# Group 0's first norm in pairs of feature tiles, with later mix loads and another home for the first projection weights

## The chip, the cores and the metric

The kernel runs on one core of one Trainium2 chip. The metric is the device time of one launch in microseconds (us); lower is better. Only one execution is profiled; the other runs give a time alone.

## The reference, cut to what matters

One layer of a streaming encoder is computed for 1024 prompt frames and 32 frames of a running stream, model width 1024. In short:

```
h   = x * (1 + sc1) + sh1                       # adaLN, sc/sh/g from the conditioning vector
... = split(h @ w_in)                           # q,k,v and gates of three head groups
mix = concat([mlstm, fox, gmlp]) @ w_o          # 4 + 8 + 4 heads of 64
x   = layer_norm(ALPHA * x + (1 + g1) * mix, ln1_g, ln1_b)
h   = x * (1 + sc2) + sh2
y   = (silu(h @ w_gate) * (h @ w_up)) @ w_down
x   = layer_norm(ALPHA * x + (1 + g2) * y, ln2_g, ln2_b)
```

All matrices are float32. The kernel works with features on the 128 partitions and frames along the free axis, so a vector of 1024 features is 8 feature tiles. It also returns keys, values, gates and states.

## The kernel before, in words

**Split products.** A float32 product is made of three matmuls (`gemm`, L111): each operand is kept as a rounded high half and a low half (hi, lo), and hi*hi, hi*lo and lo*hi are added up in PSUM. `weights` (L92) loads 512 KB of weights into one of three `raw` buffers, casts the high half on ScalarE (L104) and subtracts for the low half on VectorE (L105); the halves `whi` and `wlo` go into rings of three buffers each in the common pool `wp`, or into a pool that the caller names.

**Groups.** The frames are two groups: group 0 is frames 0 to 511, group 1 is frames 512 to 1055, the 32 stream frames last. Each group is cut into two column ranges (`MM`); for group 0 they are 0 to 255 and 256 to 511, called the first and the second range below.

**Order of the work.** After the start come the projections and the mixing heads of group 0, in an order written out by hand (`ORDER`, L42). Its last entries are the projection of attention head 7 for group 0 (`q7`, `head_unit`, L396), chunk 2 of the mLSTM, the attention of head 7 (`f7`), chunk 3 of the mLSTM (`m3`) and a gMLP unit (`G3`). `head_unit` ends with four evacuations of its bank (L408 to L413) and stores of the queries and keys to DRAM (L418, L419). Then `run` emits, from L1462:

1. `wo_mix(0, ...)` for six of the eight tiles of the concatenated mix: load a tile from DRAM (SyncE queue, L1006), cast its high half on ScalarE (L1007), subtract for its low half on VectorE (L1008). The order of tiles is `KORDER[0]` = 2, 3, 4, 6, 7, 5, 0, 1; tiles 0 and 1 hold the mLSTM's heads and come last.
2. Three projections of heads 2 to 4 for group 1 (`fm_unit`, L235, with `evac_qk`, L362).
3. `wo_mix` for the last two tiles.
4. The output projection of group 0, first range, eight output tiles m in order (`wo_range`, L1045). Weights of m = 0, 1, 2 go into a pool of their own, `pw`, which takes space that the mixing heads had; those of 3 to 7 into the common ring. Residual tiles come from DRAM in pairs (`wo_res`, L1018).
5. The second range in the order 0, 5, 6, 7, 3, 4, 1, 2, with five weights kept and those of 3 and 4 made anew, woven with the norm of the first range (`ln1`, L1083).
6. The norm of the second range, three projections of heads 5 to 7 for group 1, and then the feed-forward of group 0 (`up`, L1130), woven with the attention of group 1 (`mixers`, L1330).

**The norm.** `sublayer_end` (L1065) adds gate times projection to the residual tile z (L1074) and keeps a sum and a sum of squares; the mean of feature tile 0, found by a matmul with a constant (`ln_pivot`, L928), is taken off every tile as a pivot. `ln_stats` (L972) makes a factor r and an offset e per frame. `ln1` then does, for each feature tile k: z*r (L1091) and +e (L1092) on VectorE, an affine step on ScalarE into a buffer `tmp` (ring of four) (L1095), a cast into `hh` on ScalarE (L1099), a subtraction into `hl` on VectorE (L1100). `hh` and `hl` (`tm_ah` and `tm_al` in the profile) are what `up` multiplies. The buffer `sil`, in a ring of two, is what `up` uses for its silu (L1145).

**What orders an engine's queue.** Each engine runs its instructions in one order, fixed when the program is built: the builder simulates a timeline (L1681) and takes, by the order of the code and by priority (attention and mLSTM of group 0 have a raised one, L1451), what the simulation has ready. `tc.issue_after(x)` keeps what is written inside it behind instruction x on x's engine.

Of the kernel before, what the change touches and what calls it, by code (L numbers as in the profile page):

```python
# [7 lines left out]
F32 = mybir.dt.float32  # L8
F32R = mybir.dt.float32r
AF = mybir.ActivationFunctionType  # L10
ALU = mybir.AluOpType
# [4 lines left out]
P = 128  # L16
D = 1024
KT = 8
# [8 lines left out]
MM = (((0, 256), (256, 512)), ((0, 272), (272, 544)))  # L27
# [27 lines left out]
def weave(*parts):  # L55

    parts = list(parts)
    while parts:
        for p in list(parts):
            if next(p, parts) is parts:  # L60
                parts.remove(p)


def f(ap):
    return ap.bitcast(F32)


class Kernel:
# [17 lines left out]
        return self.lastload  # L86

    def store(self, out, in_, eng=None):
        (eng or self.nc.sync).dma_start(out, in_)


    def weights(self, src, nk, ncol, eng=None, pool=None):  # L92
# [303 lines left out]
    def head_unit(self, h):  # L396

        nc = self.nc
        w = self.weights(self.d["w_in_f"][2 + h], KT, P)
        self.phase = "head"  # L400
        k1, k2, qp, q2, v = self.heads[h] = self.head_tiles(h, 512, 512)
        self.decay(q2[64:68], h, slice(2, 6), (0, 4))
        self.decay(k2[64:68], h, slice(0, 4), (0, 4))
        self.load(f(v), self.dv[:, :4, h * P:(h + 1) * P])
        ps = self.t(self.pg, [P, 512], F32, "g")
        self.gemm(ps, w, slice(0, P), *self.h1parts(0, 512))
        lo, hi = slice(0, 64), slice(64, 128)
        nc.scalar.activation(qp[lo], ps[lo], AF.Copy, scale=0.125)  # L408
        nc.vector.scalar_tensor_tensor(qp[hi], ps[lo], 0.125, f(qp[lo]), ALU.mult, ALU.subtract)
        nc.scalar.copy(k1[hi], ps[hi])  # L410
        nc.vector.tensor_tensor(k2[lo], ps[hi], f(k1[hi]), ALU.subtract)
        nc.scalar.copy(k1[lo], ps[hi])
        nc.scalar.activation(q2[lo], ps[lo], AF.Copy, scale=0.125)  # L413
        for o in (0, 256):
            kr = self.t(self.sm, [P, 272], F32, "qkr", 2)
            nc.scalar.copy(kr[hi, :256], ps[hi, o:o + 256])
            self.store(self.d["o_kT"][h, :, o:o + 256], kr[hi, :256])
        self.store(self.dqh[h, hi, :512], f(k1[hi]))  # L418
        self.store(self.dql[h, hi, :512], f(k2[lo]))  # L419
        if h < QD:  # L420
            evac = self.evac_qk(h)
            self.phase = "fm"
            for o, n in self.ranges((1,)):
                ps = self.t(self.pg, [P, 512], F32, "g")
                self.gemm(ps[:, :n], w, slice(0, P), *self.h1parts(o, n))
                evac(o, n, ps[:, :n])
# [501 lines left out]
    def ln_pivot(self, st, z, sl):  # L928
        nc = self.nc
        ps = self.t(self.pt, [P, 512], F32, "t")  # L930
        n = sl.stop - sl.start
        nc.tensor.matmul(ps[:, :n], self.ones8, z[:, 0, sl], start=True, stop=True)
        nc.scalar.copy(st["pv"][:, sl], ps[:, :n])
        nc.vector.tensor_tensor(z[:, 0, sl], z[:, 0, sl], st["pv"][:, sl], ALU.subtract)

    def ln_sum(self, st, z, m, sl):
        nc = self.nc
# [107 lines left out]
    def wo_range(self, st, a, b, order, kept, pool):  # L1045
        nc, ko = self.nc, self.KORDER[0]
        hh, hl = self.hh[0][a], self.hl[0][a]
        st["order"] = order
        for m in order:
            self.phase = "wo0"  # L1050
            if a == 0 and m % 2 == 0:
                self.wo_res(a, b, m)
            w = kept.get(m) or self.weights(self.d["w_o"][m], KT, P, None, pool if m < 3 else None)
            if a == 0 and m in (5, 7):
                with self.tc.issue_after(self.lastload.ins):
                    for k in ((0, 4), (6, 2))[m // 7]:
                        self.wo_res(*MM[0][1], k)
            kept[m] = w
            ps = self.t(self.pg, [P, 512], F32, "g")
            self.gemm(ps[:, :b - a], [w[k] for k in ko], slice(0, P), lambda i: hh[:, ko[i], :b - a],  # L1060
                      lambda i: hl[:, ko[i], :b - a])
            self.sublayer_end(0, self.z[0], m, ps, "g1", st, a, b)
            yield

    def sublayer_end(self, c, z, m, ps, gate, st, a, b):  # L1065

        sl = slice(a, b)
        pivot = st and st["pivot"]
        less = lambda: self.nc.gpsimd.tensor_tensor(z[:, m, sl], z[:, m, sl], st["pv"][:, sl], ALU.subtract)
        if pivot and m and st["sum"]:  # L1070
            less()
        g = self.modcol(gate, m)
        for x, y, i in self.parts(c, a, b):
            self.lastz = self.nc.vector.scalar_tensor_tensor(z[:, m, x:y], ps[:, x - a:y - a], g[i], z[:, m, x:y],  # L1074
                                                             ALU.mult, ALU.add)
        if pivot and m and not st["sum"]:
            less()
        if pivot and m == 0:
            self.ln_pivot(st, z, sl)
        if st and st["sum"]:  # L1080
            self.ln_sum(st, z, m, sl)

    def ln1(self, c, st, a, b):  # L1083
        self.phase = f"lna{c}"
        nc, z, hh, hl, sl = self.nc, self.z[c], self.hh[c][a], self.hl[c][a], slice(a, b)
        r, e = self.ln_stats(st, sl)
        for k in range(KT):
            yield
            self.phase = f"lna{c}"
            zk = z[:, k, sl]  # L1090
            nc.vector.tensor_tensor(zk, zk, r, ALU.mult)  # L1091
            (nc.gpsimd if c and k % 4 == 1 else nc.vector).tensor_tensor(zk, zk, e, ALU.add)  # L1092
            h = self.t(self.p2, [P, 272], F32, "tmp", 4)[:, :b - a]
            for x, y, i in self.parts(c, a, b):
                nc.scalar.activation(h[:, x - a:y - a], z[:, k, x:y], AF.Identity, bias=self.lnb[:, k, i:i + 1],  # L1095
                                     scale=self.lng[:, k, i:i + 1])
            if c:
                self.store(self.dh[:, k, sl], h)
            nc.scalar.copy(hh[:, k, :b - a], h)  # L1099
            nc.vector.tensor_tensor(hl[:, k, :b - a], h, f(hh[:, k, :b - a]), ALU.subtract)  # L1100

    def ln1_res(self, c):

        self.phase = f"lna{c}"
        for a, b in MM[c]:
            for k in range(KT):
                zk = self.z[c][:, k, a:b]
                if RESE[c] == "p":
                    self.nc.gpsimd.tensor_scalar(zk, zk, self.colp[:, 48 + k:49 + k], self.colp[:, 56 + k:57 + k],
                                                 ALU.mult, ALU.add)  # L1110
                else:
                    self.nc.scalar.activation(zk, zk, AF.Identity, bias=self.colp[:, 56 + k:57 + k],
                                              scale=self.colp[:, 48 + k:49 + k])
# [231 lines left out]
    def run(self):  # L1345
        nc, tc, d = self.nc, self.tc, self.d
# [51 lines left out]
        sl = ExitStack()  # L1398
# [61 lines left out]
        self.p2 = self.pada = self.pool("p2")  # L1460
        self.hh, self.hl, self.z = {}, {}, {}
        self.operand(0, self.ph)  # L1462
        self.wo_mix(0, self.KORDER[0][:6])
        for h in range(QD, PRE):
            self.fm_unit(w3[2 + h], self.evac_qk(h), (1,))
        self.wo_mix(0, self.KORDER[0][6:])
# [3 lines left out]
        st = self.ln_begin(nc.vector)  # L1470
        with ExitStack() as s7:
            pw = self.pool("pw", ctx=s7)
            kept = {}
            weave(self.wo_range(st, *MM[0][0], range(KT), kept, pw))
            del kept[3], kept[4]
            weave(self.wo_range(st, *MM[0][1], (0, 5, 6, 7, 3, 4, 1, 2), kept, pw), self.ln1(0, st, *MM[0][0]))
        weave(self.ln1(0, st, *MM[0][1]))
        for h in range(PRE, 8):
            self.fm_unit(w3[2 + h], self.evac_qk(h, True), (1,))
# [10 lines left out]
        last = len(GROUPS) - 1  # L1490
        for g, (j0, nj) in enumerate(GROUPS):
# [30 lines left out]
            if g == WOB - 1:  # L1522
                st = self.ln_begin(nc.gpsimd, sum=False)
# [20 lines left out]
        for g, (j0, nj) in enumerate(GROUPS):  # L1544
# [13 lines left out]
            if g < last:  # L1558
                st = self.ln_begin(nc.gpsimd, sum=False) if g == last - 1 else None
# [3 lines left out]
        n = nj * 256  # L1563
        t = self.t(self.pz, [P, 4, n], F32R, "z0", 1)
        w = self.last_weights(((t[:, 0], t[:, 1]), (t[:, 2], t[:, 3])), (2, 3))
        act2 = dict(act)
        for half, (a, b) in enumerate(LN[1][::-1]):
# [6 lines left out]
            else:  # L1574
                h, l = (self.t(pb, [P, KT * 272], F32R, f"{x}{a}", 1) for x in ("ah", "al"))
# [117 lines left out]
```

## Time and profile before

| | us |
|---|---|
| three runs | 1363.5, 1363.7, 1365.64 |
| median of the runs | 1363.7 |
| the profiled execution: its own time | 1364.8 |
| its span, first to last instruction | 1362.7 |
| TensorE (PE) busy | 1327.6 |
| VectorE (DVE) busy | 992.2 |
| ScalarE (ACT) busy | 658.5 |
| GpSimd (POOL) busy | 227.8 |

SP is SyncE, which issues most of the DMAs; "SPq" rows are its issues. A row of the timeline has the start, the duration, the engine, the line and operation, output and inputs by the program's names, how many instructions were merged into the row and, in brackets, how long the engine had been idle and what released it. "wo_" names belong to the output projection, "lna_" to its norm, "up_" to the feed-forward, "fm_" and "head_" to the projections, "fox_" to the attention.

### The profile page before, as it was taken

How to read it: one execution, taken by the hardware profiler on the slowest of the kernel's cores; microseconds unless marked ns; L12 is line 12 of the kernel's file. 1: busy time of each engine (PE TensorE's matmuls, PEld its weight loads, DVE VectorE, ACT ScalarE, POOL GpSimd, SP SyncE). 2: the span in 40 equal slices, each digit the busy share in tenths (PEclk: the TensorE clock that was granted, in tenths of full speed). 3: DMA queues.
4: the chain of work that ended last, by engine and by line, in shares of the span. 5: the costliest groups of instructions: out<-in, count | busy, mean ns of one | idle time of the engine just before them, and what ended most of it. 6: DMA issues, size and time to landing. Idle time of an engine off the chain costs nothing.

```text
span 1362.7 us, 25189 instructions
## 1 busy us (share of the span) xinstructions
PE 1327.6 (97%) x9434; PEld 1210.1 (89%) x9434; DVE 992.2 (73%) x2127; ACT 658.5 (48%) x1312; POOL 227.8 (17%) x263
## 2 busy tenths in 40 slices
PE   7999999998999899999999999999999999999996
PEld 4898988987999777888888888999999999999995
DVE  5545654678769667786776765678988988889777
ACT  3324454455436544545445354336663554545355
POOL 0202100043234200000000000373710000000341
PEclk9999999999999899999999999999999999999999
DMA  9775555546454765454344334574596758454321
GB/s 358 257 246 164 167 193 149 179 139 197 150 188 140 202 191 173 117 156 135 105 123 119 109 105 132 155 182 124 167 254 168 201 154 222 143 173 127 98 81 66
DMA packets 120377, 221.70 MB, mean 163 GB/s; under 512 B 18740, under 2 KB 64464, under 8 KB 120256
## 3 DMA queue, kind: packets, MB, share of 16 engines
q1 hardware_dynamic: 113024, 207.55, 48.7%
q0 software_dynamic: 6032, 11.94, 5.1%
q8 instruction: 74, 1.21, 0.4%
q10 hardware_dynamic: 1200, 0.62, 0.2%
q14 instruction: 47, 0.39, 0.1%
HBM read 188.13 MB, written 51.85 MB: 176 GB/s over the span
## 4 chain that ended last, share of the span: by engine, by line
PE 86%; DVE 6%; DMA 4%; ACT 2%; issue 1%; POOL 0%; SPq 0%; DVEq 0%; ACTq 0%
PE up_g L118 5%; PE up_g L119 5%; PE up_g L117 5%; PE dn_g L117 4%; PE dn_g L119 4%; PE dn_g L118 4%; PE tm_g L284 3%; PE tm_g L285 3%; PE tm_g L286 3%; PE sup_u L119 3%; PE sup_u L117 3%; PE sup_u L118 3%; PE fox_t L819 2%; PE fm_g L117 2%; PE sup_g L118 2%; PE sup_g L119 2%
## 5 line engine op out<-in xcount | busy, mean ns | idle before, releaser
L118 PE MATMUL up_g<-tm_al,up_whi 128*128 128x512 f32 (+1 forms) x384 | 141.3, 368 | 0.5 <-DVE tm_al L1100 0.5
L117 PE MATMUL up_g<-tm_ah,up_whi 128*128 128x512 f32 (+1 forms) x384 | 141.5, 370 | 0.2
L119 PE MATMUL up_g<-tm_ah,up_wlo 128*128 128x512 f32 (+1 forms) x384 | 140.6, 366 | 0.0
L1219 ACT CAST sup_whi<-sup_raw 128x1024 fp32r<-128x1024 f32 x54 | 56.0, 1048 | 90.9 <-PE dn_u L118 47.5
L117 PEld LDWEIGHTS up_g<-tm_ah,up_whi 128*128 128x128 f32 x384 | 72.8, 190 | 12.5 <-ACT tm_ah L1099 0.6
L118 PEld LDWEIGHTS up_g<-tm_al,up_whi 128*128 128x128 f32 x384 | 73.3, 191 | 11.0 <-DVE tm_al L1100 0.7
L119 PEld LDWEIGHTS up_g<-tm_ah,up_wlo 128*128 128x128 f32 x384 | 73.3, 191 | 10.7
L792 ACT ACTIVATE fox_p<-fox_s,fox_fmx 128x384 f32<-128x384 f32 (+2 forms) x96 | 55.1, 579 | 46.7 <-DVE fox_fmx L790 38.1
L104 ACT CAST up_whi<-up_raw 128x1024 fp32r<-128x1024 f32 x50 | 52.4, 1047 | 49.7 <-PE up_g L118 18.5
L1220 DVE TENSOR_TENSOR sup_wlo<-sup_raw,sup_whi 128x1024 fp32r<-128x1024 f32 x54 | 68.2, 1267 | 10.4 <-ACT sup_whi L1219 10.3
L1074 DVE SCALAR_TENSOR_TENSOR wo_z<-dn_g,start_mod,wo_z 128x512 f32<-128x512 f32 (+4 forms) x120 | 60.3, 521 | 20.1 <-PE dn_g L119 19.8
L105 DVE TENSOR_TENSOR up_wlo<-up_raw,up_whi 128x1024 fp32r<-128x1024 f32 x50 | 65.4, 1308 | 12.1 <-ACT up_whi L104 11.4
L117 PE MATMUL dn_g<-up_acth,dn_whi 128*128 128x512 f32 (+2 forms) x200 | 74.1, 371 | 0.0
L119 PE MATMUL dn_g<-up_acth,dn_wlo 128*128 128x512 f32 (+2 forms) x200 | 73.4, 367 | 0.0
L118 PE MATMUL dn_g<-up_actl,dn_whi 128*128 128x512 f32 (+2 forms) x200 | 72.9, 365 | 0.0
L824 ACT CAST fox_pth<-fox_t 128x512 fp32r<-128x512 f32 (+1 forms) x80 | 41.1, 545 | 55.9 <-PE fox_t L819 55.8
L104 ACT CAST dn_whi<-dn_raw 128x1024 fp32r<-128x1024 f32 (+1 forms) x44 | 42.7, 970 | 51.5 <-PE dn_u L118 11.2
L787 DVE TENSOR_REDUCE fox_fmx<-fox_s 128x1 f32<-128x384 f32 (+2 forms) x96 | 52.6, 552 | 13.5 <-PE fox_s L784 12.3
L825 DVE TENSOR_TENSOR fox_ptl<-fox_t,fox_pth 128x512 fp32r<-128x512 f32 (+1 forms) x80 | 49.4, 631 | 15.7 <-ACT fox_pth L824 15.5
L105 DVE TENSOR_TENSOR dn_wlo<-dn_raw,dn_whi 128x1024 fp32r<-128x1024 f32 (+1 forms) x44 | 49.5, 1126 | 12.6 <-ACT dn_whi L104 11.8
L284 PE MATMUL tm_g<-tm_whi,start_h1h 128*128 128x256 f32 (+1 forms) x192 | 55.9, 291 | 1.8 <-DVE tm_traw L355 1.7
L285 PE MATMUL tm_g<-tm_wlo,start_h1h 128*128 128x256 f32 (+1 forms) x192 | 56.1, 292 | 0.0
(663 smaller groups left out, 4788.9 us busy)
## 6 DMA issues: line engine op xcount, KB each, us to landing
up_raw<-w_gu SPq DMA_DIRECT2D x50, 512.0 KB
dn_raw<-w_dn SPq DMA_DIRECT2D x28, 512.0 KB
ada_late<-w_ada SPq DMA_DIRECT2D x24, 512.0 KB
sup_raw<-w_gu SPq DMA_DIRECT2D x20, 512.0 KB
start_dp<-w_gu SPq DMA_DIRECT2D x19, 512.0 KB
start_dp<-w_gu POOLq DMA_DIRECT2D x19, 512.0 KB, 8.0
wo_raw<-w_o SPq DMA_DIRECT2D x18, 512.0 KB
sup_raw<-start_dp SPq DMA_DIRECT2D x18, 512.0 KB
```

Source lines behind the costliest of these rows:

```text
L104: nc.scalar.copy(hi[:, :w], raw[:, :w])
L105: (eng or nc.vector).tensor_tensor(lo[:, :w], raw[:, :w], f(hi[:, :w]), ALU.subtract)
L117: nc.tensor.matmul(ps, hi, xh(k), start=start and k == 0, stop=False)
L118: nc.tensor.matmul(ps, hi, xl(k), start=False, stop=False)
L119: nc.tensor.matmul(ps, lo, xh(k), start=False, stop=stop and k == n - 1)
L284: nc.tensor.matmul(ps[:, :ncol], xh, hi, start=k == 0, stop=False)
L285: nc.tensor.matmul(ps[:, :ncol], xh, lo, start=False, stop=False)
L787: nc.vector.tensor_reduce(mxs[:, x:x + 1], s[:, :w], AX.X, ALU.max, negate=True)
L792: nc.scalar.activation(pr[:, lo:hi], banks[x][:, :hi - lo], AF.Exp, bias=mxs[:, 0:1], accum_out=sums[:, x:x + 1])
L1074: self.lastz = self.nc.vector.scalar_tensor_tensor(z[:, m, x:y], ps[:, x - a:y - a], g[i], z[:, m, x:y], ALU.mult, ALU.add)
L1219: nc.scalar.copy(h, x)
L1220: tt(l, x, f(h), ALU.subtract)
```

## The change

Three things change.

- The first norm of group 0 goes through a new function, `ln1_pairs`, two feature tiles per VectorE instruction: z*r and +e on 512 columns, two affine steps of 256 columns on ScalarE, one cast and one subtraction of 512 columns. The product of a pair is kept behind the sum of the pair before. The buffer between is `sil` instead of `tmp`.
- The loads of the first six mix tiles are kept behind the last store of head 7's projection on SyncE's queue.
- The weights of m = 0, 1, 2 go into the common ring and those of 3, 4, 5 into `pw`. The second range goes 2, 6, 7, 3, 4, 5, 0, 1, with 0 and 1 made anew; the pivot is the first tile in this order instead of tile 0, and the residual loads follow the new order.

```diff
     def store(self, out, in_, eng=None):
-        (eng or self.nc.sync).dma_start(out, in_)
+        return (eng or self.nc.sync).dma_start(out, in_)
...
         self.store(self.dqh[h, hi, :512], f(k1[hi]))
-        self.store(self.dql[h, hi, :512], f(k2[lo]))
+        self.lastq = self.store(self.dql[h, hi, :512], f(k2[lo]))
...
-            w = kept.get(m) or self.weights(self.d["w_o"][m], KT, P, None, pool if m < 3 else None)
+            w = kept.get(m) or self.weights(self.d["w_o"][m], KT, P, None, pool if 3 <= m < 6 else None)
             if a == 0 and m in (5, 7):
                 with self.tc.issue_after(self.lastload.ins):
-                    for k in ((0, 4), (6, 2))[m // 7]:
+                    for k in ((2, 6), (4, 0))[m // 7]:
                         self.wo_res(*MM[0][1], k)
...
-        if pivot and m and st["sum"]:
+        first = st and m == st["order"][0]
+        if pivot and not first and st["sum"]:
             less()
...
-        if pivot and m == 0:
-            self.ln_pivot(st, z, sl)
+        if pivot and first:
+            self.ln_pivot(st, z[:, m], sl)
...
         r, e = self.ln_stats(st, sl)
+        if c == 0:
+            yield from self.ln1_pairs(z, hh, hl, sl, r, e)
+            return
...
+    def ln1_pairs(self, z, hh, hl, sl, r, e):
+        nc, n = self.nc, sl.stop - sl.start
+        two = lambda x: x.unsqueeze(1).to_broadcast([P, 2, n])
+        last = None
+        for k in range(0, KT, 2):
+            yield
+            self.phase = "lna0"
+            zk = z[:, k:k + 2, sl]
+            with self.tc.issue_after(last.ins) if last else ExitStack():
+                nc.vector.tensor_tensor(zk, zk, two(r), ALU.mult)
+            last = nc.vector.tensor_tensor(zk, zk, two(e), ALU.add)
+            h = self.t(self.p2, [P, 544], F32, "sil", 2)[:, :2 * n].rearrange("p (k n) -> p k n", k=2)
+            for i in range(2):
+                nc.scalar.activation(h[:, i], zk[:, i], AF.Identity, bias=self.lnb[:, k + i, 0:1],
+                                     scale=self.lng[:, k + i, 0:1])
+            nc.scalar.copy(hh[:, k:k + 2, :n], h)
+            nc.vector.tensor_tensor(hl[:, k:k + 2, :n], h, f(hh[:, k:k + 2, :n]), ALU.subtract)
...
-        self.wo_mix(0, self.KORDER[0][:6])
+        with tc.issue_after(self.lastq.ins):
+            self.wo_mix(0, self.KORDER[0][:6])
...
-            del kept[3], kept[4]
-            weave(self.wo_range(st, *MM[0][1], (0, 5, 6, 7, 3, 4, 1, 2), kept, pw), self.ln1(0, st, *MM[0][0]))
+            del kept[0], kept[1]
+            weave(self.wo_range(st, *MM[0][1], (2, 6, 7, 3, 4, 5, 0, 1), kept, pw), self.ln1(0, st, *MM[0][0]))
```

More of the change, by code (lines that the diff above doesn't have):

```diff
@@ L931, in ln_pivot @@
         n = sl.stop - sl.start
-        nc.tensor.matmul(ps[:, :n], self.ones8, z[:, 0, sl], start=True, stop=True)
+        nc.tensor.matmul(ps[:, :n], self.ones8, z[:, sl], start=True, stop=True)
         nc.scalar.copy(st["pv"][:, sl], ps[:, :n])
-        nc.vector.tensor_tensor(z[:, 0, sl], z[:, 0, sl], st["pv"][:, sl], ALU.subtract)
+        nc.vector.tensor_tensor(z[:, sl], z[:, sl], st["pv"][:, sl], ALU.subtract)
     def ln_sum(self, st, z, m, sl):
@@ L1075, in sublayer_end @@
                                                              ALU.mult, ALU.add)
-        if pivot and m and not st["sum"]:
+        if pivot and not first and not st["sum"]:
             less()
-        if pivot and m == 0:
-            self.ln_pivot(st, z, sl)
+        if pivot and first:
+            self.ln_pivot(st, z[:, m], sl)
         if st and st["sum"]:
```

## The prediction, on record before the changed kernel ran

> **What bounds the kernel now.** I read the page's busy times first, then TensorE's waits in the part that the change touches, then a table of stretches around each wait.
>
> ```profile
> span 1362.7 us, 25189 instructions
> PE 1327.6 (97%) x9434; PEld 1210.1 (89%) x9434; DVE 992.2 (73%) x2127; ACT 658.5 (48%) x1312; POOL 227.8 (17%) x263
> ```
>
> TensorE stands still for 35.1 us of the span (1362.7 - 1327.6). Nothing but those 35.1 us, and time in which its clock was low, can be won without taking matmuls away, and the change takes none away. TensorE's waits from 300 to 480 us:
>
> ```profile
> PE fox_s L783 <- DMA fox_k<-start_dqh: 3.8, 1, 3.8
> PE fox_s L783 <- ACT head_k L412: 3.0, 1, 3.0
> PE wo_t L932 <- DVE wo_z L1074: 1.7, 1, 1.7
> PE tm_g L284 <- DVE tm_traw L355: 1.7, 1, 1.7
> PE up_g L118 <- DVE tm_al L1100: 0.5, 1, 0.5
> ```
>
> The fourth, of a gMLP bank, isn't touched; the other four sum to 9.0 us. Columns of the next table that matter: stretch, its length, PE busy, and after the five engines the granted PE clock, DMA share and GB/s.
>
> ```profile
> 330.80:333.90 3.10, 0.06 (x2) 0.01 (x1) 3.01 (x8) 3.00 (x8) 0.31 (x1) 1.00 0.99 374
> 335.00:339.00 4.00, 4.00 (x21) 4.00 (x22) 3.81 (x18) 1.96 (x8) 0.00 (x0) 0.58 0.60 193
> 380.30:382.00 1.70, 0.01 (x1) 0.01 (x1) 1.68 (x3) 1.41 (x2) 0.00 (x0) 1.00 1.07 383
> 382.00:449.00 67.00, 66.91 (x540) 66.15 (x540) 56.13 (x113) 34.72 (x72) 26.72 (x26) 1.00 0.46 141
> ...
> 455.40:459.30 3.90, 0.14 (x2) 0.03 (x1) 0.03 (x1) 0.00 (x0) 0.91 (x2) 0.90 0.97 235
> 459.30:465.30 6.00, 6.00 (x25) 5.81 (x26) 1.47 (x7) 1.84 (x3) 0.00 (x0) 0.50 1.11 221
> ...
> 600.00:1300.00 700.00, 699.79 (x4857) 656.12 (x4856) 551.03 (x1032) 347.84 (x627) 109.52 (x111) 1.00 0.53 148
> ```
>
> Two of the three large waits are followed by a low clock: 4 us at 0.58 cost 4 * 0.42 = 1.7 us, 6 us at 0.50 cost 3.0 us. The wait of 1.73 us at 380.3 is not: the clock is 1.00 behind it. So a wait that shrinks enough returns more than its length. From 600 to 1300 us TensorE is busy 699.8 of 700 us at full clock: whatever is saved before 470 us moves the end by as much, unless later work is ordered anew.
>
> **Part one: mix loads behind head 7's last store.** The wait at 330.8 is for L412, the fourth evacuation of head 7's bank. ScalarE, then VectorE, then SyncE:
>
> ```profile
> 328.71 1.14 ACT L1007 CAST tm_ah<-tm_al 128x512 fp32r<-128x512 f32 x2
> 330.39 0.58 ACT L410 CAST head_k<-head_g 64x512 fp32r<-64x512 f32 x1 [0.54 <-DVE head_qp L409]
> ...
> 332.03 1.14 ACT L1007 CAST tm_ah<-tm_al 128x512 fp32r<-128x512 f32 x2
> ...
> 333.27 0.57 ACT L412 CAST head_k<-head_g 64x512 fp32r<-64x512 f32 x1
> ```
> ```profile
> 327.88 1.76 DVE L105 TENSOR_TENSOR fm_wlo<-fm_raw,fm_whi 128x1024 fp32r<-128x1024 f32 x1
> 329.67 0.68 DVE L409 SCALAR_TENSOR_TENSOR head_qp<-head_g,head_qp 64x512 fp32r<-64x512 f32 x1
> ...
> 331.05 1.27 DVE L1008 TENSOR_TENSOR tm_al<-tm_al,tm_ah 128x512 fp32r<-128x512 f32 x2
> ...
> 332.44 0.69 DVE L411 TENSOR_TENSOR head_k<-head_g,head_k 64x512 fp32r<-64x512 f32 x1
> ```
> ```profile
> 324.91 2.44 SPq L85 DMA_DIRECT2D tm_al<-start_dmix x5
> ...
> 333.16 0.47 SPq L89 DMA_DIRECT2D start_dql<-head_k x1
> ```
>
> Five mix loads were issued at 324.9, so their casts and subtractions stand inside the chain L409, L410, L411, L412. Kept behind the store of 333.16, none of them can. L410 still waits for L409, which stands behind a weight subtraction until 329.67; so the chain starts no sooner. L411 then follows L410 at about 331.0 instead of 332.44 and L412 at about 331.7 instead of 333.27: the 3.0 us wait becomes about 1.5 us, a gain of **1.5 us** (bounds: 0 if other work takes the place, 3.0). The remaining 1.5 us is nearest to the 1.73 us wait, behind which the clock stayed full, so I add the **1.7 us** of low clock (bounds 0 and 1.7).
>
> The moved work is five loads, five casts of 0.57 us on ScalarE and five subtractions of 0.64 us on VectorE. SyncE's queue loses the 2.4 us of issues ahead of two weight loads and gets them back behind the store. They are hidden as long as the last mix tile is ready in time, which chunk 3 of the mLSTM sets; VectorE's last low half, and TensorE's first matmul of the projection:
>
> ```profile
> 372.90 1.00 DVE L1008 TENSOR_TENSOR tm_al<-tm_al,tm_ah 128x512 fp32r<-128x512 f32 x1 [0.18 <-ACT tm_ah L1007]
> ```
> ```profile
> 374.45 0.28 PE L117 MATMUL wo_g<-tm_ah,wo_whi 128*128 128x256 f32 x1
> ```
>
> The last two tiles are seventh and eighth in the sum, 18 matmuls behind 374.45; at 66.91/540 = 0.124 us a matmul that is 376.7, against 373.9: 2.8 us of cover. TensorE comes about 3 us earlier, so this chain must come earlier too; most of it hangs on TensorE's own order and does.
>
> **Part two: weights of m = 0, 1, 2 in the common ring.** ScalarE, VectorE and SyncE:
>
> ```profile
> 362.36 0.49 ACT L369 ACTIVATE fm_qkh<-fm_g,start_qsc 128x272 fp32r<-128x272 f32 x1 [2.17 <-PE fm_g L119]
> ...
> 366.73 2.94 ACT L104 CAST wo_whi<-wo_raw 128x1024 fp32r<-128x1024 f32 x3
> ...
> 379.24 1.05 ACT L104 CAST wo_whi<-wo_raw 128x1024 fp32r<-128x1024 f32 x1 [5.98 <-DMA wo_raw<-w_o]
> ```
> ```profile
> 380.32 1.23 DVE L105 TENSOR_TENSOR wo_wlo<-wo_raw,wo_whi 128x1024 fp32r<-128x1024 f32 x1 [6.00 <-ACT wo_whi L104]
> 381.46 0.48 DVE L1074 SCALAR_TENSOR_TENSOR wo_z<-wo_g,start_mod,wo_z 128x256 f32<-128x256 f32 x1
> ```
> ```profile
> 371.27 0.41 SPq L85 DMA_DIRECT2D wo_raw<-w_o x1
> ```
>
> The casts for m = 0, 1, 2 wait for the mixers' space until 366.7. Only then are the raw buffers free, m = 3 is loaded from 371.27 and lands at 379.2, and VectorE, in order, stands 6.0 us before m = 3's subtraction with the evacuation of m = 0 (L1074) behind it; TensorE waits for that with the pivot matmul, 1.7 us. In the ring m = 0 takes the place of head 2's weights, whose last matmul ended by 362.4: cast and subtraction are done by about 364.7 (1.05 + 1.23), and m = 3 loads some 6 us sooner. Nothing is late next: m = 2 takes head 4's place, free at 374.4, is ready by 376.7 and is used two units behind 374.45 (48 * 0.124 = 6.0, so 380.4). I take the whole **1.7 us** (bounds 0 and 1.7). The count of weight loads, casts and subtractions stays ten; the new order of the second range only changes which two are made anew. The first range's TensorE work shows no other wait (66.91 of 67.00 us), so nothing more is to be had there.
>
> **Part three: the norm in pairs.** VectorE in the norm of the second range, the group row of the affine steps, and SyncE's longest wait from 440 to 465 us:
>
> ```profile
> 442.52 2.76 DVE L1091 TENSOR_TENSOR wo_z<-wo_z,wo_pv 128x256 f32<-128x256 f32 x8
> ...
> 445.87 0.50 DVE L370 SCALAR_TENSOR_TENSOR fm_qkl<-fm_g,start_qsc,fm_qkh 128x272 fp32r<-128x272 f32 x1
> ...
> 454.48 0.95 DVE L1100 TENSOR_TENSOR tm_al<-lna_tmp,tm_ah 128x256 fp32r<-128x256 f32 x2
> ```
> ```profile
> L1095 ACT ACTIVATE lna_tmp<-wo_z,wo_lnb,wo_lng 128x256 f32<-128x256 f32 x16 | 9.2, 596 | 4.7 <-DVE wo_qs L949 3.2 <-DVE wo_z L1092 1.5
> ```
> ```profile
> SPq L85 <- DMA o_kT<-fm_qkr: 3.1, 1, 3.1
> ```
>
> All eight products come first (0.345 us each), then the sums, so the last low half ends at 455.4, 12.9 us after the start. 24 instructions of 256 columns at 0.345 us are 8.3 us; 12 of 512 columns at 0.64 us (the subtractions above) are 7.6 us. The real gain is order: product, sum, two affine steps (0.6 us each), cast (0.57) and subtraction give the first pair after 0.64 * 3 + 1.2 + 0.57 = 3.7 us, at 446.2; the 0.5 us wait for the first low half goes (**0.5 us**). VectorE's other work in the stretch is 12.9 - 8.3 = 4.6 us at most, so the last pair ends by 442.5 + 7.6 + 3 = 453.1 if 3 of these 4.6 us fall inside.
>
> TensorE then has the rest of the first feed-forward unit ready earlier, but at 455.4 it stops for another reason: head 0's scores stand next in its order and wait for `fox_k`. Those loads wait for the store of the last projected keys, whose evacuation (L370) runs at 445.87 between norm instructions. What pairs can move there is work from behind the scores to before them: the last two feature tiles of two units, 12 matmuls, 12 * 0.124 = **1.4 us**. Bounds: -1.5 us (a chain evacuated two 512-column instructions later) to 3.8 us (no wait left). The remaining 2.4 us lies midway between 1.73 (no low clock) and 3.0 (low clock); I keep the 3.0 us of low clock as lost.
>
> Cost on the other side: `sil` is a ring of two that `up` shares. Its first silu must now wait for the third pair's subtraction, about 450.5. The bank behind it comes free later by up to 4 us. Before, TensorE stands at the scores then, so I price it at 0; uncovered it costs up to 4 us.
>
> Sum: 1.5 + 1.7 + 1.7 + 0.5 + 1.4 = 6.8 us. Against the profiled execution, 1364.8, that is 1358.0; that execution is 1.1 us over the runs' median of 1363.7, so I say **1356.9**.
>
> **Rivals.**
> - *The second low clock goes too* (1353.9). The rows leave open where between 1.73 and 3.0 us of wait the clock falls. If 2.4 us is below that point, 3.0 us more are won. For it: 1.73 was free. Against: 3.0 was not. The Trainium skill (TensorE: Matmul & The Clock Gate, section "What's actually happening") says that the clock halves after an idle window of about 3.4 us, free-running. By that rule 2.4 us can't fill a window and the time would be this one; the trace agrees on the halving (0.50), and its fall behind 3.0 us, with another wait just before, is short of that figure. Chance 0.20.
> - *The waits only move* (1361.7). Each engine's order is fixed by a simulated timeline, and new work in VectorE's and ScalarE's queues can fill the place of the mix casts. Then part two's 1.7 and 0.3 us elsewhere remain. Chance 0.24, some 0.14 of it within 0.2%.
> - *The deferred mix tiles come late* (1368.5, slower). Behind 333 us the loads meet a DMA that is full (share 0.99, 374 GB/s); there m = 3's load took 8 us (371.27 to 379.2). If the five take 8 us as well, their casts, in order, hold up attention 7 and mLSTM chunk 3 by about 8 us. From 2.8 us of delay on, the projection starts late: 8 - 2.8 = 5.2 us and a low clock of 3.0; part one wins nothing, parts two and three 3.6: 4.6 us slower. Against: head 7's attention has raised priority, and TensorE has a gMLP unit and three projections to run meanwhile. Chance 0.16.
>
> **How the numbers follow.** Forecast 1356.9 with 0.40 (its own range 1355 to 1360), rivals 0.20, 0.24, 0.16. Faster by over 0.2% (2.7 us, about what a measurement tells here): 0.40 + 0.20 + 0.10 = 0.70; within: 0.14; slower: 0.16. The range goes from 1350.5 (rival one and the 3.0 us bound of part one, with 2 us of the scores' wait) to 1365.0, which leaves out most of the slower case.
>
> **What would show each step.** Right: no mix cast before head 7's four evacuations; the wait for L412 near 1.5 us and full clock behind it; no 6 us of VectorE before m = 3's subtraction and no wait of the pivot matmul; products of 512 columns followed by their sums, a first low half some 4 us into the norm. Wrong: a wait at the first projection for mix tiles, a wait of `up` for `sil` or its bank, a scores' wait as long as before or longer, or new TensorE idle time between 465 and 600 us.

## The result, and the profile after

The changed kernel takes 1361.9 us in the median of 12 runs (1357.4 to 1365.5), the kernel before 1364.7 us in 12 runs of the same chip. The ratio is 0.9973 with a 95% interval of 0.9961 to 0.9985: faster by 3.7 us (2.0 to 5.3), where 6.8 us were forecast; the two medians themselves are 2.8 us apart. The direction and the wide range (1350.5 to 1365.0) held, the forecast's own range (1355 to 1360) did not: the sum was too large.

The first trace of the changed kernel (1365.5 us with a span of 1363.0, its slowest run of the twelve) answers to the lines shown of before. Page, span and busy times, columns as before:

```profile
span 1363.0 us, 25152 instructions
...
PE 1331.5 (98%) x9434; PEld 1210.4 (89%) x9434; DVE 991.3 (73%) x2103; ACT 659.0 (48%) x1304; POOL 231.8 (17%) x263
```

TensorE stands still for 31.5 us instead of 35.1, but it is busy for 3.9 us more with the same 9434 matmuls: part of them ran at a low clock. TensorE's waits in the changed kernel from 300 to 520 us (us in total, times, longest):

```profile
PE tm_g L284 <- DVE tm_traw L355: 1.8, 1, 1.8
PE tm_g L724 <- DVE tm_tmsum L300: 1.6, 1, 1.6
PE wo_g L117 <- ACT tm_ah L1007: 1.4, 2, 1.2
PE up_g L117 <- ACT up_whi L104: 1.1, 1, 1.1
PE up_g L117 <- DVE up_sil L1172: 0.8, 1, 0.8
PE up_g L119 <- DVE up_wlo L105: 0.5, 1, 0.5
PE fox_s L783 <- DMA foxs_k<-start_dsf: 0.5, 1, 0.5
PE wo_g L118 <- DVE tm_al L1008: 0.3, 1, 0.3
```

Where TensorE waited 3.0 us for head 7's bank it now waits 1.6 us, and for another result: a gMLP matmul (L724) stands first and waits for VectorE's L300. The evacuation that it waited for (L412) ends 0.2 us later, at 332.93. ScalarE, VectorE and TensorE of the changed kernel:

```profile
332.36 0.57 ACT L412 CAST head_k<-head_g 64x512 fp32r<-64x512 f32 x1
```
```profile
332.33 0.41 DVE L300 TENSOR_TENSOR tm_tmsum<-tm_g,tm_tmsum 32x256 f32<-32x256 f32 x1
```
```profile
332.80 0.63 PE L724 MATMUL tm_g<-tm_gvn,start_wsp 32*32 32x64 f32 x8 [1.57 <-DVE tm_tmsum L300]
```

The pivot matmul's wait (1.7) is gone and that of the scores for `fox_k` (3.8) all but gone. New are the first projection's waits for mix tiles (1.4 and 0.3 us) and the feed-forward's for its weights (1.1, 0.5) and for the evacuation of a silu bank (0.8).

The norm of the second range runs in the order that was meant: a product (L1115), its sum (L1116), and the low half (L1122), each for two tiles. VectorE, with the first and the last low half:

```profile
439.31 0.68 DVE L1115 TENSOR_TENSOR wo_z<-wo_z,wo_pv 128x512 f32<-128x512 f32 x1
...
441.13 0.68 DVE L1116 TENSOR_TENSOR wo_z<-wo_z,wo_qs 128x512 f32<-128x512 f32 x1
...
445.08 0.68 DVE L1122 TENSOR_TENSOR tm_al<-lna_sil,tm_ah 128x512 fp32r<-128x512 f32 x1
...
451.87 0.90 DVE L1122 TENSOR_TENSOR tm_al<-lna_sil,tm_ah 128x512 fp32r<-128x512 f32 x1 [1.07 <-ACT tm_ah L1121]
```

The loads of head 0's keys, before and in the changed kernel (the feed-forward's first matmul starts at 443.14 and 444.68):

```profile
454.56 1.17 SPq L85 DMA_DIRECT2D fox_k<-start_dqh  x2
```
```profile
452.53 1.18 SPq L85 DMA_DIRECT2D fox_k<-start_dqh  x2
```

One trace doesn't size these waits, so there are two of the kernel before and three of the changed one (the runs are told below). The three stretches that hold parts one, two and three, in the first and the second trace of the kernel before (stretch, length, PE busy first; then the other engines, the granted PE clock, DMA share, GB/s):

```profile
300.00:345.00 45.00, 40.30 (x308) 36.44 (x307) 39.57 (x121) 24.44 (x65) 14.22 (x20) 0.96 0.64 203
345.00:430.00 85.00, 83.21 (x684) 81.55 (x684) 63.63 (x131) 36.16 (x68) 30.04 (x34) 1.00 0.51 163
430.00:520.00 90.00, 84.98 (x552) 71.96 (x552) 60.52 (x145) 53.06 (x122) 12.27 (x15) 0.96 0.67 191
```
```profile
300.00:345.00 45.00, 40.27 (x298) 36.28 (x298) 38.83 (x119) 24.64 (x66) 13.95 (x20) 0.92 0.61 197
345.00:430.00 85.00, 84.93 (x699) 83.37 (x698) 65.16 (x136) 36.34 (x70) 30.04 (x35) 1.00 0.51 166
430.00:520.00 90.00, 83.56 (x555) 69.67 (x554) 60.82 (x147) 53.21 (x122) 12.22 (x15) 1.00 0.66 193
```

The same view of the changed kernel, its three traces in order:

```profile
300.00:345.00 45.00, 41.66 (x320) 37.83 (x319) 39.57 (x120) 24.57 (x65) 14.23 (x20) 0.96 0.66 203
345.00:430.00 85.00, 83.15 (x663) 81.08 (x662) 62.58 (x124) 38.92 (x71) 31.56 (x34) 0.96 0.47 150
430.00:520.00 90.00, 87.07 (x564) 71.87 (x563) 61.21 (x130) 50.85 (x112) 16.16 (x15) 0.98 0.73 206
```
```profile
300.00:345.00 45.00, 41.99 (x320) 37.97 (x320) 39.73 (x120) 25.16 (x67) 14.27 (x20) 0.96 0.66 203
345.00:430.00 85.00, 83.02 (x675) 81.44 (x674) 64.31 (x126) 39.40 (x70) 34.82 (x35) 0.98 0.49 154
430.00:520.00 90.00, 88.01 (x565) 71.91 (x565) 62.11 (x137) 51.04 (x113) 14.45 (x14) 1.00 0.74 209
```
```profile
300.00:345.00 45.00, 41.99 (x322) 37.98 (x321) 39.83 (x120) 25.16 (x67) 14.26 (x20) 0.96 0.65 203
345.00:430.00 85.00, 83.62 (x691) 82.02 (x689) 66.39 (x131) 40.73 (x72) 37.04 (x37) 1.00 0.50 158
430.00:520.00 90.00, 87.54 (x572) 71.12 (x572) 61.89 (x137) 50.73 (x112) 12.40 (x12) 1.00 0.72 209
```

Idle time is length minus PE busy, the price of a low clock is (1 - clock) times length (two digits of the clock make a price of 1.7 us read as 1.8, and 3.4 as 3.6). In means over the traces, us:

| stretch (part) | idle, before to after | low clock, before to after | change | forecast |
|---|---|---|---|---|
| 300 to 345 (one) | 4.7 to 3.1 | 2.7 to 1.8 | -2.5 | -3.2 |
| 345 to 430 (two) | 0.9 to 1.7 | 0 to 1.7 | +2.5 | -1.7 |
| 430 to 520 (three) | 5.7 to 2.5 | 1.8 to 0.6 | -4.4 | -1.9 |

Together that is -4.4 us, inside the measured interval. In its stretch part two lost what it was to win, and in the third the gain was more than twice part three's term.

### The profile page after: what moved, and what is told of

Same layout as the page of the kernel before. It is cut to its first block, busy times and chain, and to the rows that moved or that the text cites. A ratio compares the mean times of both kernels' runs of the same rounds, so it can differ in the third digit from the quotient of the medians.

```text
span 1363.0 us, 25152 instructions
## 1 busy us (share of the span) xinstructions
PE 1331.5 (98%) x9434; PEld 1210.4 (89%) x9434; DVE 991.3 (73%) x2103; ACT 659.0 (48%) x1304; POOL 231.8 (17%) x263
## 4 chain that ended last, share of the span: by engine, by line
PE 87%; DVE 5%; DMA 4%; ACT 1%; issue 1%; SPq 1%; POOL 1%; ACTq 0%; DVEq 0%
PE up_g L119 6%; PE up_g L117 5%; PE up_g L118 5%; PE dn_g L117 4%; PE dn_g L119 4%; PE dn_g L118 4%; PE tm_g L284 3%; PE tm_g L285 3%; PE tm_g L286 3%; PE sup_u L119 3%; PE sup_u L117 3%; PE sup_u L118 3%; PE wo_g L118 2%; PE fox_t L819 2%; PE wo_g L119 2%; PE wo_g L117 2%
## 5 line engine op out<-in xcount | busy, mean ns | idle before, releaser
L105 DVE TENSOR_TENSOR up_wlo<-up_raw,up_whi 128x1024 fp32r<-128x1024 f32 x50 | 66.7, 1334 | 14.1 <-ACT up_whi L104 13.2
```

The lines of the kernel that those rows point to most:

```text
L105: (eng or nc.vector).tensor_tensor(lo[:, :w], raw[:, :w], f(hi[:, :w]), ALU.subtract)
```

## The experiments

All times below are medians against runs of the kernel before on the same chip; a difference of two variants is known to 2 to 3 us. The theories stood thus. **A**: the gain is taken back at the first output projection, because its last two mix tiles come late. **B**: no new wait matters, and each part gives what it removes by itself. **C** (first round): time saved before 600 us is given back later. Later texts define their own letters anew.

**Each part alone.** Only the hunks of one part are applied.

```diff
# e1
-        self.wo_mix(0, self.KORDER[0][:6])
+        with tc.issue_after(self.lastq.ins):
+            self.wo_mix(0, self.KORDER[0][:6])
# e2, with the new order of the second range and the pivot that goes with it
-            w = kept.get(m) or self.weights(self.d["w_o"][m], KT, P, None, pool if m < 3 else None)
+            w = kept.get(m) or self.weights(self.d["w_o"][m], KT, P, None, pool if 3 <= m < 6 else None)
# e3
+        if c == 0:
+            yield from self.ln1_pairs(z, hh, hl, sl, r, e)
+            return
```

> Part one alone: the first six mix loads behind head 7's last store, all else as before. Theory A (the gain of the parts is taken back at the first output projection, because the mix tiles 0 and 1 now come late): TensorE's wait for head 7's evacuation falls from 3.0 to about 1.6 us, but TensorE then waits 0.4 to 2 us for mix tiles in the first projection; time 0 to 2 us under before. Rival B (no new wait; each part gives what it removes): the wait falls as well, none follows, 3 us under before. Rival C (all that is saved before 600 us is given back later, by the attention of group 1): no difference in time.

> Part two alone: weights of m = 0, 1, 2 in the common ring, those of 3, 4, 5 in the pool of their own, the second range in the new order. All theories: the 1.7 us wait of the pivot matmul is gone. A: no wait for mix tiles, since TensorE comes no earlier; 1.7 us under before, give or take 1. B: the same. C: no difference in time.

> Part three alone: the norm of group 0 in pairs. A and B: the wait of head 0's scores for their keys falls from 3.8 us to 2.4 us or less, and a wait of the feed-forward for its silu's bank of up to 1 us is new; 1.5 to 5 us under before, the 5 with the low clock behind the scores gone. C: the same waits, no difference in time, since the attention of group 1 ends later.

**Parts in company.** The same hunks, two parts at a time.

> Parts one and two, the norm as before. Part one alone gave -1.6 us, part two alone +4.5. Theory A (part two loses only because, without part one, the mix loads and ring weights meet, and the sums on GpSimd then fall beside VectorE's adds): with the loads deferred the loss is gone; about 1362.5 us, no VectorE add over 1.5 us in the first projection, and TensorE's wait for mix tiles 0 and 1 at the first projection (1.7 us) is there as in the changed kernel. Rival B (part two loses by itself, the parts add up): about 1367.5 us, and a VectorE add of over 3 us beside GpSimd's sums again. Rival C (part three is what heals it): as B, 1366 to 1368, with waits behind 470 us.

> Parts one and three, the first projection's weights as before. Theory A (part two's wait of 1.7 us at the pivot matmul was worth having away, but its place was taken by 1.7 us for mix tiles): the pivot wait shows here with 0.7 to 1.8 us or the mix wait does, and the time is that of the changed kernel within 1.5 us, 1360 to 1363. Rival B (the parts add up): 1.9 us less than before, 1362.9, and 1.8 us more than the changed kernel. Rival D (part two is a loss in every company): 1358 to 1359, faster than the changed kernel.

> Parts two and three, the mix loads as before. Theory A (part two needs part one): slower, 1367 to 1370, with the wait for head 7's bank at 3 us or more and TensorE's waits for VectorE in the first projection. Rival B (the parts add up): +4.2 us, 1369. Rival C (part three heals it): 1362 to 1364.

Measured (us is the ratio's distance from 1 times 1364.7):

| parts | ratio, 95% interval | us |
|---|---|---|
| one (e1) | 0.9988 [0.9978, 0.9998] | -1.6 |
| two (e2) | 1.0033 [1.0021, 1.0044] | +4.5 |
| three (e3) | 0.9998 [0.9986, 1.0011] | -0.3 |
| one, two (e5) | 1.0011 [0.9997, 1.0026] | +1.5 |
| one, three (e6) | 0.9991 [0.9976, 1.0005] | -1.2 |
| two, three (e7) | 0.9989 [0.9974, 1.0004] | -1.5 |
| all (the change) | 0.9973 [0.9961, 0.9985] | -3.7 |

Part one gives -1.6, -3.0, -0.9 and -2.2 us in its four companies: some 2 us in the mean. Parts one and three add up as far as such differences tell (-1.6 and -0.3 against -1.2 together). Parts two and three don't: part two costs 4.5 or 3.1 us without the pairs and wins 1.2 or 2.5 with them, which is about the limit of what can be told; the pairs give -0.3 and +0.4 without part two, -6.0 and -5.2 with it. That ends theory B. No theory had seen the loss of e2, where all expected 1.7 us less or no difference, nor that e3 would win nothing although its scores' wait fell to 0.4 us; e1 met theory A's time (0 to 2 us less) without A's wait for mix tiles. Part of part two's own loss can be read in its trace, where VectorE, then GpSimd, in the first projection, and TensorE's wait that follows, are:

```profile
390.27 0.48 DVE L1075 SCALAR_TENSOR_TENSOR wo_z<-wo_g,start_mod,wo_z 128x256 f32<-128x256 f32 x1 [1.51 <-POOL wo_z L1069]
390.79 3.86 DVE L947 TENSOR_TENSOR wo_zs<-wo_z 128x256 f32<-128x256 f32 x1
394.57 0.47 DVE L1075 SCALAR_TENSOR_TENSOR wo_z<-wo_g,start_mod,wo_z 128x256 f32<-128x256 f32 x1
```
```profile
389.49 4.87 POOL L1069 TENSOR_TENSOR wo_z<-wo_z,wo_pv 128x256 f32<-128x256 f32 x7
```
```profile
PE wo_g L117 <- DVE wo_z L1075: 2.8, 3, 1.3
```

One VectorE addition of 256 columns, 0.41 us elsewhere in that trace, lasts 3.86 us while GpSimd runs seven subtractions back to back; the evacuation behind it is late, and TensorE waits 2.8 us for banks. The same 3.86 us stands in e7's trace, and in no trace with part one: where the mix loads are deferred, part two doesn't meet it. The pairs don't remove it; in e7 they win elsewhere. In e3, the pairs alone, the scores' wait goes too, yet others take its place (430 to 520 us):

```profile
PE up_g L117 <- ACT start_qks L380: 1.3, 1, 1.3
PE fox_t L819 <- DVE fox_p L800: 1.1, 1, 1.1
PE fox_o L827 <- DVE fox_ptl L825: 1.0, 1, 1.0
PE up_g L117 <- DVE up_sil L1171: 0.7, 1, 0.7
PE fox_s L783 <- DMA fox_k<-start_dqh: 0.4, 1, 0.4
```

From 430 to 520 us TensorE idles 5.0 us in e3 and 6.3 in e6, as in the kernel before, and 2.6 us in e7. So the pairs pay only together with part two. What differs is when the keys come. With the pairs alone the first load of head 0's keys goes out 10.7 (e3) and 10.5 us (e6) after the feed-forward's first matmul, no sooner than in the two traces of the kernel before (11.4 and 10.7), and the scores start 15.8 and 16.0 us after that matmul (before: 16.1 and 15.5): TensorE has 16 matmuls more behind it by then, but over the stretch it idles as long. With part two without the pairs (e2, e5, e11) the load goes out 9.9 to 10.0 us after it. With both (e7 and the three traces of the changed kernel) it does so 7.6 to 8.5 us after it, and the scores start at 13.2 to 14.4 us. Why the builder's order brings the keys sooner only with both parts wasn't found.

**Tile 5's cast behind chunk 3's copy** (e4). In the changed kernel ScalarE, in order, waited for tile 5's load with chunk 3's copy behind it.

```diff
-    self.wo_mix(0, self.KORDER[0][:6])
+    self.wo_mix(0, self.KORDER[0][:5])
+with tc.issue_after(self.lastmt.ins):   # lastmt: chunk 3's copy, L702
+    self.wo_mix(0, self.KORDER[0][5:6])
```

> The changed kernel, with mix tile 5's load, cast and subtraction kept behind the copy of mLSTM chunk 3's result on ScalarE. Theory A: chunk 3's copy no longer stands behind a cast that waits for a load; its store is some 1.5 us earlier, TensorE's waits for mix tiles in the first projection (1.7 us in the changed kernel) fall below 0.5 us and the low clock behind them goes; 2 to 5 us under the changed kernel, ratio to before 0.993 to 0.996. B and C: ratio as that of the changed kernel, 0.997.

Measured: 1360.2 us, 0.9974 [0.9963, 0.9985], as the changed kernel; the waits for mix tiles stay at 1.0 and 0.3 us. Theory A's 0.5 us or less isn't met: the store does go out 3.7 us after tile 5's load was issued, against 4.6 to 5.1 in the three traces of the changed kernel, but the next load follows it only after 3.3 us. ScalarE's order alone isn't what makes the tiles late.

**The weight load of m = 3 kept late** (e9; e10 with the norm's own ring; e11 without pairs). In the changed kernel, SyncE's queue around chunk 3's store, and ScalarE's casts of the last mix tiles:

```profile
363.16 0.32 SPq L85 DMA_DIRECT2D tm_al<-start_dmix  x1
363.57 0.39 SPq L85 DMA_DIRECT2D wo_raw<-w_o  x1
...
368.23 0.37 SPq L89 DMA_DIRECT2D start_dmix<-mlstm_mtot  x1
371.81 0.32 SPq L85 DMA_DIRECT2D tm_al<-start_dmix  x1
```
```profile
367.31 0.62 ACT L1007 CAST tm_ah<-tm_al 128x512 fp32r<-128x512 f32 x1 [2.79 <-DMA tm_al<-start_dmix]
367.83 0.37 ACT L702 COPY mlstm_mtot<-mlstm_t 128x256 f32<-128x256 f32 x1
...
374.89 0.62 ACT L1007 CAST tm_ah<-tm_al 128x512 fp32r<-128x512 f32 x1 [4.03 <-DMA tm_al<-start_dmix]
```

The load of m = 3's weights (512 KB) now goes out at 363.57, 0.4 us behind tile 5's load. Tile 5's cast starts 4.2 us after its load was issued (3.7 and 3.8 in the other two traces); chunk 3's copy stands behind that cast, the store of 368.23 behind the copy, and the load that needs that store follows 3.6 us behind it (2.4 and 2.3 in the other two traces).

```diff
+    if a == 0 and m == 3:
+        late.enter_context(self.tc.issue_after(self.lastmix.ins))   # the last mix load
+        late.enter_context(self.tc.issue_after(self.firstz.ins))    # m = 0's evacuation
     w = kept.get(m) or self.weights(self.d["w_o"][m], ...)
```

> The changed kernel, but the load of the projection weights for m = 3 (512 KB, issued at 363.6 in the changed kernel, ahead of mLSTM chunk 3's store) is kept behind the last mix load on SyncE's queue, and its subtraction behind the evacuation of m = 0 on VectorE. Theory E (that early load, which part two makes possible, shares the DMA with mix tile 5, with chunk 3's store and so with the last two mix loads, and that is TensorE's new wait of 1.7 us at the first projection): the store reaches memory and the next mix load is issued within 2 us of it, not 3.6; the wait for the mix tiles falls below 0.5 us; 1.5 us less than the changed kernel in idle time, 1358 to 1360.5 in all. Rival F (the last two tiles are late for another reason, such as the residual loads or ScalarE's order): the wait stays at 1.2 us or more and the time within 1 us of the changed kernel. Rival G (the late load brings the wait at the pivot matmul back): a wait for m = 0's evacuation or for m = 3's weights of 1 us or more; 1361 to 1364.

> The same late load together with the pairs' own ring of four. If the two waits are separate (theory E, and a small gain from the ring): 0.5 us less than with the late load alone, 1357.5 to 1360. If TensorE's wait behind the scores takes back what comes early (as part one alone gave back 3.1 us between the first feed-forward unit and the second): no less than the late load alone, 1359 to 1362.

> Parts one and two with the late load, the norm as before the change. Theory E and parts that add up from there: the wait for mix tiles (3.2 us with parts one and two) falls below 0.5 us, and the time goes from 1366.9 to 1363 to 1364.5. Theory C (part two is a loss wherever the norm isn't in pairs, whatever the load does): 1365.5 to 1367.5, with TensorE's waits from 430 to 520 us still near 5.9 us.

In e9, tile 5's load goes out at 362.22. ScalarE's cast of it, SyncE's queue, and TensorE's waits from 345 to 430 us:

```profile
365.18 0.62 ACT L1007 CAST tm_ah<-tm_al 128x512 fp32r<-128x512 f32 x1 [1.59 <-DMA tm_al<-start_dmix]
```
```profile
366.10 0.37 SPq L89 DMA_DIRECT2D start_dmix<-mlstm_mtot  x1
368.28 0.32 SPq L85 DMA_DIRECT2D tm_al<-start_dmix  x1
```
```profile
PE wo_g L119 <- DVE wo_wlo L105: 0.6, 1, 0.6
PE wo_g L118 <- DVE tm_al L1008: 0.3, 1, 0.3
PE wo_g L117 <- ACT tm_ah L1007: 0.3, 1, 0.3
```

The cast starts 3.0 us after the load was issued (2.9 in e10 and e11, 2.8 in e1 and e6, which have no early weight load either), and the waits for mix tiles fall from 1.4 to 2.0 us (the three traces of the changed kernel) to 0.6, in e11 from 3.2 (e5) to 0.3. So theory E names their cause, the early weight load, but the way is tile 5's slower load: from the store to the next load it is 2.2 us, against 2.3 and 2.4 in two of the changed kernel's traces. Theory E's time failed. That of e9 is the changed kernel's, 1361.4 us, 0.9972 [0.9960, 0.9983], not 1358 to 1360.5: a wait for the late weights (0.6) and waits behind 430 us (idle 3.6 us there, against 2.5) stand in the place of the old one. e10 gave 1361.7, 0.9974 [0.9962, 0.9987]. The time of e11 is 1364.6 us, 0.9997 [0.9983, 1.0010], against 1.0011 in e5, which is less than such a difference can tell.

**The norm's own ring** (e8). The pairs' affine steps, casts and subtractions go tile by tile through the ring `tmp` instead of `sil`.

```diff
-            h = self.t(self.p2, [P, 544], F32, "sil", 2)[:, :2 * n]...
             for i in range(2):
+                h = self.t(self.p2, [P, 272], F32, "tmp", 4)[:, :n]
```

> The changed kernel, but the pairs' affine results, casts and subtractions go tile by tile through the norm's own ring of four instead of the ring of two that the feed-forward's silu shares; products and sums stay pairs. Theory A (the silu ring holds the feed-forward back): the wait of 0.8 us at 454 for the silu's bank is gone, and those of 1.1 and 0.5 us for feed-forward weights at 475 shrink with the low clock behind them; 1 to 3 us less than the changed kernel, 1358 to 1360. Rival B (these waits come from the number of instructions on ScalarE and VectorE, not from the ring): 4 casts and 4 subtractions more make them longer; 1361 to 1364.

Measured: 1361.8 us, 0.9976 [0.9965, 0.9987]; `up_g` still waits for `up_sil` (1.0 and 0.3 us). The ring isn't what delays that evacuation. Here only 74 matmuls of the feed-forward stand before the scores (80 in the kernel before, 96 in the changed one), the keys' loads go out 6.6 us after the first of them, and the time is the changed kernel's all the same.

**Pairs without the order** (e12). The wait of a product for the sum of the pair before it is left out.

```diff
-            with self.tc.issue_after(last.ins) if last else ExitStack():
-                nc.vector.tensor_tensor(zk, zk, two(r), ALU.mult)
+            nc.vector.tensor_tensor(zk, zk, two(r), ALU.mult)
```

> The changed kernel without the rule that a pair's product waits in VectorE's order until the sum of the pair before it is done; the pairs themselves stay. If the gain of part three is the order (as the prediction has it): products come first again, the first low half 2 us later, a wait of up to 1 us for it and the scores' wait longer than 1 us; 1 to 3 us more than the changed kernel, 1363 to 1365. If it is only the smaller number of instructions: 1361 to 1362.5.

Measured: 1365.2 us, 0.9996 [0.9983, 1.0008], so the order is worth some 3 us (0.9996 against 0.9973). What the smaller number of instructions gives can't be told: e12 is 2.0 us under e5, which has no pairs. TensorE's waits behind 430 us:

```profile
PE fox_s L783 <- DMA fox_k<-start_dqh: 2.8, 1, 2.8
PE up_g L117 <- ACT fm_qkr L372: 1.0, 1, 1.0
```

In e12 72 matmuls of the feed-forward's first products stand before the scores, in the kernel before 80, in the changed kernel 96 (by the records). The keys' loads go out 8.4 us after the first of them, as in the changed kernel; so the 24 matmuls, 24 * 0.124 = 3.0 us, are what the order moves, and the scores' wait grows by 2.3 to 2.5 us without it.

**The same kernels traced again** (e13, e14: the changed kernel; e15: the kernel before; one run each).

> The changed kernel once more, for a second trace of it. If a low clock belongs to the wait ahead of it: again 0.64 and 0.77 behind the wait at 333 us and 0.50 to 0.73 from 378 to 386, some 6.6 us in all. If it belongs to the execution: TensorE's waits are the same to 0.1 us each (8.1 us from 300 to 520 us), and at least one of the three low stretches is missing or stands elsewhere.

> As the run before it, a third trace of the changed kernel: the same two readings.

> The kernel before once more, for a second trace. If the low clock belongs to the wait: 1.7 us behind the wait for head 7's bank and 3.6 us behind the scores' wait again. If it belongs to the execution: the two waits are 3.0 and 3.8 us again, and one of the low stretches is missing or another is there.

They took 1361.2, 1359.2 and 1363.7 us; their stretches are quoted above. Neither reading held whole. Behind the wait at 333 us the low clock is there in all three traces of the changed kernel; behind the mix tiles it costs 3.4, 1.7 and 0 us; behind the scores of the kernel before 3.6 and 0. And not every wait repeats: the first projection of the kernel before idles 1.8 us in one trace and 0.1 in the other.

## Why the prediction was partly right

**Part one held, in part by luck.** TensorE's wait went to 1.6 us, as worked out (1.5): L409 to L412 take 2.9 us from the start of the one to the end of the other, where they took 4.2. It now ends with L300, which the working didn't have. The 1.7 us of low clock is right as a mean only, and by luck: the term had the clock full behind the wait. In the 300 to 345 us stretch of all traces, five without part one (the kernel before twice, e2, e3, e7) show a clock of 0.96 or 0.92, that is 1.8, 3.6, 3.6, 1.8 and 3.6 us; of twelve with part one (the changed kernel three times, e1, e4 to e6, e8 to e12) eight show 0.96 and four 1.00. The means are 2.9 and 1.2 us.

**Part two is the step that failed**: "Nothing is late next", and with it "the whole 1.7 us". The pivot wait did go. But "m = 3 loads some 6 us sooner" was counted as a gain only. That load goes out 7.7 us sooner, is 512 KB and passes the DMA beside tile 5's load, with chunk 3's copy, its store and the last two mix loads behind that tile; the 2.8 us of cover for these two was worked out without it. Instead of -1.7 the stretch gave +0.8 us of idle time and +1.7 us of low clock. The rival "the deferred mix tiles come late" had the place right. Its cause, the five deferred loads, isn't enough by itself (e1 and e6 have them and show no wait for mix tiles), and neither is the early weight load (e2 and e7 have it, 2.4 us behind tile 5's load, and show none): it took both. Besides, the 1.7 us to be won was a size of one trace; the second shows 0.1.

**Part three was mis-sized, and the parts were added up as if they were separate.** The order was a gain, as put, and e12 shows it. But three things came out otherwise. The first low half is done 6.1 to 6.5 us into the norm, not 3.7, because VectorE has other work and waits in between, and the norm lasts 13.1 to 13.6 us where 10.6 were worked out (442.5 to 453.1; before: 12.9). It ends earlier all the same, 8.0 to 8.5 us behind the feed-forward's first matmul and not 12.3, because it begins 5.1 to 5.4 us ahead of that matmul and not 0.6. Then 16 matmuls moved to before the scores, not 12. And the keys' arrival, which the term took as fixed, moved too: their loads go out 7.8 to 8.5 us after that matmul instead of 10.7 to 11.4, which the pairs bring only together with part two. So the scores' wait fell to 0.3 to 0.5 us, not to 2.4: -3.2 us of idle time for a term of 1.9 (0.5 + 1.4), and 1.2 us of low clock in the mean where it was kept as lost. In this company part two, a loss in its own stretch, is worth some 2.5 us (e6 against the change, about what such a difference can tell). The `sil` ring priced at 0 did no harm (e8); the evacuation of the first bank is late all the same, at 0.8 us, which had no term. The waits for feed-forward weights (0.4 to 1.6 us) had none either.

**The rivals.** "The waits only move" put 2.0 us on the change, at 1361.7 us. That time was met partly because the kernel before ran 1.0 us slower beside the changed one (1364.7) than in its first three runs (1363.7), and the way was another: not part one's wait but part two's moved. It is in line with e4, e8, e9 and e10, which each change one of the new waits and all stay at ratios of 0.9972 to 0.9976. What sets that floor is open. Theory C has no support: from 520 to 1340 us TensorE idles about 1.0 us or less in every trace. Two sums of the prediction are slightly off without effect: 4.6 us over 1363.7 is 1368.3, not 1368.5, and the range's lower end comes to 1350.4.

## What to carry to other kernels

A load that gets an earlier slot is an added transfer at that time: list the stores and loads of every due chain that passes the DMA then, before it is counted as a gain. Judge a part in the company it will run in; here the same hunk cost 4.5 us alone and won some 2.5 us with the rest. When work is moved ahead of a wait, ask whether the end of the wait moves as well. Before a term is taken from a wait of 2 us, look at a second trace of the same kernel.

## What the hardware showed

**The low clock comes in steps and by chance.** Summed over slices of 1 us, its price in one of the three stretches is 0 or a multiple of 1.7 us in every trace (3.3 in e2, where the last window reaches past 520). The three traces of the changed kernel have 6.8, 3.4 and 1.7 us of it from 300 to 520 us and spans of 1363.0, 1359.3 and 1357.4 us, so the low clock makes 5.1 of the 5.6 us between the first span and the last. With part one TensorE waits at about 328 and 333 us, for 1.3 to 2.2 and 1.6 us (e11 has only the first, 1.8 us). That brought a step in eight traces of twelve, e11 among them, and none in e1 (1.3 and 1.6 us), e8, e10 and e12 (1.7 and 1.6), whose two waits are as long. The Trainium skill (TensorE: Matmul & The Clock Gate, section "What's actually happening") says that the clock halves after an idle window of some 3.4 us and that these windows run freely. The trace agrees in the step (3.4 us at half clock cost 1.7) and in the chance; here waits well short of such a window were enough, in some executions.

**GpSimd can shut VectorE out for a row of instructions.** The addition of 3.86 us above outlasts five of GpSimd's seven subtractions (4.87 / 7 = 0.70 us each). The Trainium skill (SBUF — State Buffer, section "SBUF: two separate sides") says that the port the two share is an exclusive lock, held for a whole instruction. By that rule the addition would get its turn after one subtraction, some 0.7 us; in e2 and e7 it got none until the row ended. It isn't always so: in the kernel before, such a row took 6.05 us and VectorE's additions beside it 0.46 us each. What decides wasn't found.
